# Matmuls of constants, read by nobody, put among the last steps of a layer's mixing stage

## The chip, the cores and the metric

The kernel runs on one core of one Trainium2 chip. The metric is the device time of one execution in microseconds (us). Three executions of the kernel before took 1523.73, 1532.48 and 1538.41 us; the median, 1532.48 us, is the time before.

## The reference

One layer of a hybrid decoder, on 1024 prompt tokens and 8 single tokens that continue older sequences (decode tokens); all tensors are float32. In short:

```
h    = rms_norm(x) ; proj = h @ w_in
y_r  = rwkv7_mix(proj[:, :1792])             # 8 heads of 64: a state matrix per head, updated token by token
y_s  = attention over the last 128 tokens    # 4 query heads, 2 key heads, relative bias, a learned sink
y_m  = attention into 256 memory tokens      # 4 heads
x    = x + concat(y_r, y_s, y_m) @ w_out
x    = x + square(relu(rms_norm(x) @ w_ff1)) @ w_ff2
```

The prompt's attention is computed in blocks of 128 queries. The decode tokens take the same steps with their own state, key and value caches. Outputs are x for all tokens, the new states and the new caches.

## The kernel before

**Stages.** `layers` computes the norm, all projections, the recurrent heads and both attentions, and writes the results of the heads to DRAM (`mixs`); `merge` and `out_proj` load them and multiply by `w_out`; `ffn` does the two large products (`pq` in the trace). Large matmuls split each float32 operand in two parts (tag `w`, `hbig`, `mix`) and take three matmuls for one. The smaller ones are plain float32 matmuls; the trace shows each of these as two MATMUL records.

**The program.** The order of the work in `layers` is written out by hand: the text `PROG` (L35) is a list of steps, and `program` (L407) calls them one after another. `D`, `Q`, `V` are projections. The recurrent heads are 8 units (4 head pairs by 2 halves of the tokens), and each goes through `L F P I W M C N`: load, front, products, inversion of small triangular blocks on GpSimd (L590), values, merge of the inverse (L625), the chain over 8 chunks (L662), and finish (L685; it holds two plain float32 matmuls of 128x128 by 512 columns, `g<-tmp,cst` and `g<-sg,lg`). `A` takes one step of the prompt's attention: 16 steps have work, called units A1 to A16 here. A1 to A8 attend to the memory, A9 to A16 to the window. `R` and `T` take one step of the decode tokens' recurrence (L924) and attention (L1042).

**One attention unit** (`att_unit`, L863) computes the scores of two query blocks in two PSUM buffers of tag `d` (8 matmuls, `d<-mk,qi` and `d<-mkl,qi`, or `d<-kT,qi` and `d<-kTl,qi`), takes the softmax with VectorE and ScalarE, transposes the weights into a buffer of tag `g` (`g<-cst,pe`), copies them out (`pts`) and multiplies with the values. Tag `d` has two buffers, `g` has four, `cx` and `cy` one each (`ps`, L92). A buffer comes free when the last reader of what it held is done.

**Who sets the order.** Each engine executes its own queue in order. The queues are filled by a planner at build time (L1598): a list scheduler that follows a model of the machine, takes the ready instruction that is first in the program, and lets a later one go ahead when an earlier one has to wait for data or for a buffer.

**The decode tokens' attention** uses the tags `cx` and `cy` and two SBUF buffers `d4` (tile `d` in the DMA rows) for its caches, which are loaded one after another.

Of the kernel before, what the change touches and what calls it, by code (L numbers as in the profile page):

```python
# [16 lines left out]
T = 1032  # L17
# [17 lines left out]
PROG = """  # L35
    D12 D13 D8 D0 B G X D4 D6 L0 F0 P0 D5 L1 F1 P1 D10 D1 I0 W0 M0 D9 L2 I1 D2 F2 C0 P2 L3 W1 M1 I2
    C1 N0 F3 P3 D3 W2 M2 L4 N1 F4v P4 C2 D7 I3 V D11 W3 M3 Y I4v Q0 N2 Q1 C3 L5 F5 P5 W4 L6 M4 C4 Q2
    N3 F6v I5 Q3 W5 P6 M5 N4 L7 K C5 F7d A I6 A P7 A W6 M6 R R I7 R R R W7 N5 Av Av C6 Av M7 Av A Av
    N6 C7 T T A T Av T A A N7 A Av Av A R T T T Avc T T
"""  # L40


class K:
# [363 lines left out]
    def program(self, steps):  # L407

        U = [(p, h) for p in range(4) for h in range(2)]
        unit = {"L": self.loads, "F": self.front, "P": self.products, "I": self.invert, "W": self.values,  # L410
                "M": self.merge_inv, "C": self.chain, "N": self.finish}
        self.at = (x for i in (2, 3, 0, 1) for b in range(2) for x in self.attention(i, b))
        self.dt = "cx"
        gen = {"A": self.at, "R": self.decode_rwkv(), "T": self.decode_attn()}
        one = {"B": self.memory, "G": self.bias_tables, "X": self.open_units, "V": self.kv_in, "Y": self.keys, "K": self.open_attn}
        for s in steps.split():
            n = int(s[1:].strip("vdc") or 0)
            self.alt = self.nc.vector if "v" in s else self.nc.gpsimd
            self.gt = "d" if "d" in s else "g"
            self.st = ("cx", "cy") if "c" in s else ("d", "d")  # L420
            if s[0] in unit:
                unit[s[0]](*U[n])
            elif s[0] == "D":
                self.rw_in(n, {12: ("d", "d", "g"), 13: ("cy", "cx", "g")}.get(n, "ddd"))
            elif s[0] == "Q":
                self.q_in(n)
            elif s[0] in gen:
                next(gen[s[0]], None)
            else:
                one[s[0]]()  # L430

    def layers(self):
        self.f = {}
        pool = self.pool
        self.mixs = self.dp.tile([8, 128, TP], F32, name="mixs")
        self.xs = self.dp.tile([12, 128, TP], F32, name="xs")
        self.rk = self.dp.tile([4, 128, TP], F32, name="rk")
        with pool("rows", "left") as self.rp:
            self.xw, self.sg = self.tl("xw", [128, TP]), self.tl("sg", [128, TP])

            self.early = [pool("start", "left"), pool("mem", "left")]
            self.sp = self.early[0].__enter__()
            self.startup()
            self.ep = self.early[1].__enter__()
            self.program(PROG)
            self.apool.__exit__(None, None, None)
            self.dma(self.O["shift"], self.sout)
            self.upool.__exit__(None, None, None)
# [1153 lines left out]
```

## Time and profile before

| | |
|---|---|
| median of 3 runs (lowest, highest) | 1532.48 us (1523.73, 1538.41) |
| profiled execution: its own time, its span | 1522.56 us, 1520.8 us |
| mean granted TensorE clock over the span | 0.919 |
| TensorE matmuls (PE), busy | 1380.5 us, 91% |
| TensorE weight loads (PEld), busy | 1273.3 us, 84% |
| VectorE, GpSimd, ScalarE, busy | 952.4, 754.2, 564.4 us |

The span is the time from the first to the last instruction; 1.8 us of the execution lie around it. The page cuts the span in 40 slices of 38 us and gives, for each, the busy share of each engine in tenths and the TensorE clock that was granted, in tenths of full speed. [...] The attention units, the decode tokens and the last recurrent units run from about 527 to 719 us.

### The profile page before, as it was taken

The numbers are of one execution on the slowest core, as the hardware profiler recorded it, in microseconds if no ns is written. First come the engines' busy times: TensorE is split into PE (matmuls) and PEld (weight loads), VectorE is DVE, ScalarE is ACT, GpSimd is POOL, SyncE is SP. The second block draws the span as 40 slices with busy tenths as digits, with TensorE's granted clock in tenths as the row PEclk, the third lists the DMA queues.
The fourth block names the chain that finished last, engine by engine and source line by source line (L and its number), as shares of the span: only waits on it lengthen the run. The fifth ranks groups of instructions, "written<-read, shape, count | busy, mean of one in ns | idle before, by whom it ended". The sixth has DMA issues, their size and how long they took to land. (4 is left out here: it accounts for less than half of the span.)

```text
span 1520.8 us, 29414 instructions
## 1 busy us (share of the span) xinstructions
PE 1380.5 (91%) x11391; PEld 1273.3 (84%) x11391; DVE 952.4 (63%) x1704; ACT 564.4 (37%) x1057; POOL 754.2 (50%) x905
## 2 busy tenths in 40 slices
PE   5898899989899599896997899999999899999998
PEld 5887797769787477563997799999999899999998
DVE  7658466657766655974446877777777643328830
ACT  6433223223233144343444343344244554423430
POOL 7113563461143655450236565566556555678862
PEclk9899899999889667677998899999999999999999
DMA  6154323314434632336522345545565986469850
GB/s 236 61 164 128 86 71 101 106 49 120 125 108 114 175 82 47 83 100 212 212 84 83 118 173 204 208 165 197 202 215 185 366 319 197 148 221 310 285 168 35
DMA packets 152071, 238.18 MB, mean 157 GB/s; under 512 B 40851, under 2 KB 63340, under 8 KB 151788
## 3 DMA queue, kind: packets, MB, share of 16 engines
q1 hardware_dynamic: 132892, 191.77, 38.7%
q10 hardware_dynamic: 13824, 37.98, 6.8%
q0 software_dynamic: 5216, 6.56, 2.0%
q8 instruction: 89, 1.46, 0.4%
q14 instruction: 50, 0.41, 0.1%
HBM read 165.22 MB, written 72.08 MB: 156 GB/s over the span
## 5 line engine op out<-in xcount | busy, mean ns | idle before, releaser
L85 PE MATMUL pq<-hf,w 128*128 128x258 f32 x2688 | 325.6, 283 | 4.8 <-POOL w L53 2.0
L85 PEld LDWEIGHTS pq<-hf,w 128*128 128x128 f32 x2688 | 324.2, 190 | 6.1 <-POOL w L53 2.5
L53 POOL TENSOR_TENSOR w<-wf,w 128x512 fp32r<-128x512 f32 x130 | 209.0, 1614 | 125.8 <-ACT w L76 112.3
L85 PE MATMUL d<-hbig,w 128*128 128x344 f32 (+2 forms) x1296 | 222.2, 327 | 19.7 <-ACT w L76 9.4
L85 PEld LDWEIGHTS d<-hbig,w 128*128 128x128 f32 x1296 | 202.8, 200 | 32.8 <-ACT w L76 10.6
L53 POOL TENSOR_TENSOR w<-st,w 128x512 fp32r<-128x512 f32 x96 | 153.8, 1630 | 89.2 <-ACT w L76 89.2
L76 ACT CAST w<-wf 128x512 fp32r<-128x512 f32 x190 | 116.6, 617 | 190.2 <-PE pq L85 93.2
L76 ACT CAST w<-st 128x512 fp32r<-128x512 f32 x96 | 59.5, 620 | 222.8 <-DVE st L53 198.3
L53 DVE TENSOR_TENSOR hf<-t,hf 128x1032 fp32r<-128x1032 f32 x56 | 94.0, 1722 | 55.6 <-ACT hf L76 55.6
L53 DVE TENSOR_TENSOR st<-wf,wf 128x512 f32<-128x512 f32 x80 | 85.1, 1073 | 67.6 <-DMA wf<-in_w_ff 59.3
L85 PE MATMUL pq<-xy,w 128*128 128x258 f32 x768 | 103.9, 299 | 18.9 <-DVE t L53 16.4
L85 PEld LDWEIGHTS pq<-xy,w 128*128 128x128 f32 x768 | 101.2, 204 | 22.1 <-DVE t L53 18.3
L53 POOL TENSOR_TENSOR inv<-inv,blk 128x54 f32<-128x54 f32 (+24 forms) x217 | 70.4, 324 | 51.6 <-DMA inv<-in_winit 28.6
L85 PE MATMUL pq<-xe,w 128*128 128x258 f32 x768 | 94.4, 282 | 0.5 <-ACT w L76 0.5
L85 PEld LDWEIGHTS pq<-xe,w 128*128 128x128 f32 x768 | 92.8, 189 | 0.8 <-ACT w L76 0.8
L85 PE MATMUL pq<-xf,w 128*128 128x258 f32 x576 | 76.0, 289 | 9.2 <-DVE xf L53 6.0
L53 POOL TENSOR_TENSOR inv<-inv,inv 128x54 f32<-128x54 f32 (+24 forms) x217 | 75.8, 349 | 15.9
L85 PEld LDWEIGHTS pq<-xf,w 128*128 128x128 f32 x576 | 72.7, 195 | 10.7 <-DVE xf L53 6.8
L53 DVE TENSOR_TENSOR t<-pq,t 128x516 f32<-128x516 f32 x112 | 74.9, 685 | 8.7 <-PE pq L85 7.2
L85 PE MATMUL pq<-xa,w 128*128 128x258 f32 x576 | 73.2, 284 | 2.4 <-DVE t L53 2.4
L85 PEld LDWEIGHTS pq<-xa,w 128*128 128x128 f32 x576 | 71.0, 190 | 2.9 <-DVE t L53 2.8
L73 ACT ACTIVATE t<-t 128x1032 f32<-128x1032 f32 x64 | 67.8, 1065 | 12.2 <-DVE t L53 11.6
(404 smaller groups left out, 2452.9 us busy)
## 6 DMA issues: line engine op xcount, KB each, us to landing
wf<-in_w_ff SPq DMA_DIRECT2D x208, 256.0 KB
t<-hs SPq DMA_DIRECT2D x56, 516.0 KB
hs<-t ACTq DMA_DIRECT2D x48, 516.0 KB
wf<-in_w_in SPq DMA_DIRECT2D x34, 256.0 KB
tmp<-xs SPq DMA_DIRECT2D x32, 256.0 KB
wf<-s2s SPq DMA_DIRECT2D x32, 256.0 KB
x<-in_xT SPq DMA_DIRECT2D x8, 516.0 KB
xs<-xs SPq DMA_DIRECT2D x24, 172.0 KB
```

The costliest lines, as they stand in the source:

```text
L53: return (e or self.nc.vector).tensor_tensor(out, a, b, op=op)
L73: return self.nc.scalar.activation(out, a, f, **k)
L76: return self.nc.scalar.copy(out, a)
L85: return self.nc.tensor.matmul(out, l, r, start=start, stop=stop, **k)
```

## The change

`PROG` gets a new step `J`, put 45 times between the steps from the first `A` to the end, and `J` calls a new function `fill`: one plain float32 matmul of 128x128 by 512 columns. Its operands are columns of `cst`, a tile of constants loaded at the start, and its result goes to a new PSUM buffer of tag `d` that nobody reads.

```diff
-    N3 F6v I5 Q3 W5 P6 M5 N4 L7 K C5 F7d A I6 A P7 A W6 M6 R R I7 R R R W7 N5 Av Av C6 Av M7 Av A Av
-    N6 C7 T T A T Av T A A N7 A Av Av A R T T T Avc T T
+    N3 F6v I5 Q3 W5 P6 M5 N4 L7 K C5 F7d A J I6 J A J P7 J A J W6 J M6 J R J R J I7 J R J R J R J W7 J N5 J Av J Av J C6 J Av J M7 J Av J A J Av J 
+     N6 J C7 J T J T J A J T J Av J T J A J A J N7 J A J Av J Av J A J R J T J T J T J Avc J T J T J 
...
+        one = {"B": self.memory, "G": self.bias_tables, "X": self.open_units, "V": self.kv_in, "Y": self.keys, "J": self.fill, "K": self.open_attn}
...
+    def fill(self):
+
+        self.mm(self.ps("d"), self.cst[:, 0:128], self.cst[:, 0:512])
```

Counted along the text, the fills stand behind the attention units so: 2 behind A1, 2 behind A2, 11 behind A3, then 1, 2, 2, 1, 1, 5, 2, 2, 1, 2, 1, 1 behind A4 to A15, and 9 behind A16. The two `A` after A16 have no work.

## Rows read from the trace of the kernel before

**Rows 1.** The page: busy time of TensorE, and its clock in 40 slices.

```profile
PE 1380.5 (91%) x11391; PEld 1273.3 (84%) x11391; DVE 952.4 (63%) x1704; ACT 564.4 (37%) x1057; POOL 754.2 (50%) x905
...
PEclk9899899999889667677998899999999999999999
```

**Rows 2.** Windows: length; busy (count) of PE, PEld, DVE, ACT, POOL; clock; DMA; GB/s.

```profile
527.85:531.27 3.42, 2.96 (x13) 1.86 (x12) 2.24 (x6) 0.00 (x0) 2.72 (x10) 1.00 0.16 63
531.27:551.75 20.48, 20.48 (x78) 15.25 (x78) 7.35 (x26) 7.41 (x21) 14.94 (x35) 0.50 0.27 69
...
565.40:568.81 3.41, 3.41 (x48) 2.75 (x44) 2.52 (x9) 1.27 (x4) 1.75 (x2) 0.50 0.43 133
...
572.23:592.71 20.48, 20.48 (x119) 17.52 (x121) 7.41 (x21) 5.91 (x23) 13.97 (x46) 0.50 0.10 21
592.71:609.77 17.06, 15.43 (x168) 11.95 (x164) 14.16 (x34) 8.10 (x23) 5.81 (x17) 1.00 0.31 73
609.77:616.60 6.83, 6.83 (x70) 5.50 (x66) 6.58 (x14) 0.64 (x2) 0.72 (x1) 0.50 0.28 77
...
630.25:647.32 17.07, 11.32 (x43) 7.53 (x44) 15.23 (x31) 6.37 (x21) 8.09 (x9) 0.50 0.22 48
647.32:664.39 17.07, 16.93 (x134) 11.72 (x132) 13.93 (x31) 7.25 (x23) 11.51 (x11) 1.00 0.42 125
664.39:681.45 17.06, 16.54 (x78) 11.22 (x77) 12.47 (x62) 9.01 (x28) 8.84 (x11) 0.50 0.36 98
681.45:701.93 20.48, 16.87 (x189) 10.19 (x188) 12.13 (x33) 8.49 (x24) 0.23 (x1) 1.00 0.35 113
701.93:722.41 20.48, 10.82 (x60) 6.08 (x61) 7.01 (x20) 7.03 (x18) 0.00 (x0) 0.50 0.78 280
...
527.85:692.00 164.15, 152.59 (x1169) 112.78 (x1168) 115.05 (x293) 69.60 (x215) 81.75 (x159) 0.74 0.29 76
```

**Rows 3.** TensorE's timeline (start, length): float32 matmuls of 512 columns begun at half clock.

```profile
525.72 2.07 PE L85 MATMUL g<-sg,lg 128*128 128x512 f32 x2
...
590.11 2.02 PE L85 MATMUL g<-tmp,cst 128*128 128x512 f32 x2
592.06 1.43 PE L90 MATMUL g<-cst,y 64*64 64x64 f32 x32
...
646.53 1.42 PE L85 MATMUL g<-tmp,cst 128*128 128x512 f32 x2
...
679.56 1.92 PE L85 MATMUL g<-tmp,cst 128*128 128x512 f32 x2
```

**Rows 4.** The same view: such a matmul at full clock, and what follows it.

```profile
593.42 1.12 PE L85 MATMUL g<-sg,lg 128*128 128x512 f32 x2
594.38 0.33 PE L85 MATMUL cx<-sv,F 128*128 128x64 f32 x2
```

**Rows 5.** The same view: score matmuls at full clock, then at half clock.

```profile
599.21 0.38 PE L85 MATMUL d<-mkl,qi 64*128 64x256 f32 x1
599.52 0.38 PE L85 MATMUL d<-mk,qi 128*128 128x256 f32 x1
...
611.02 0.58 PE L85 MATMUL d<-mk,qi 128*128 128x256 f32 x1
611.53 0.58 PE L85 MATMUL d<-mkl,qi 64*128 64x256 f32 x1
```

**Rows 6.** The same view: A4's scores, a decode step written ahead of A4, A4's transposes.

```profile
555.53 0.38 PE L85 MATMUL d<-mk,qi 128*128 128x256 f32 x1
...
577.15 1.66 PE L85 MATMUL g<-xd,lw 64*128 64x8 f32 x7
...
594.77 1.48 PE L89 MATMUL g<-cst,pe 128*128 128x128 f32 x12
```

**Rows 7.** Timelines of VectorE (A11's scores read) and TensorE (A12's begun).

```profile
646.77 1.66 DVE L70 SCALAR_TENSOR_TENSOR pe<-d,nrq,bias 128x256 f32<-128x256 f32 x4 [1.48 <-PE g L89]
...
649.43 0.36 PE L85 MATMUL d<-kT,qi 128*128 128x256 f32 x1
```

More of the change, by code (lines that the diff above doesn't have):

```diff
@@ L37 @@
     C1 N0 F3 P3 D3 W2 M2 L4 N1 F4v P4 C2 D7 I3 V D11 W3 M3 Y I4v Q0 N2 Q1 C3 L5 F5 P5 W4 L6 M4 C4 Q2
-    N3 F6v I5 Q3 W5 P6 M5 N4 L7 K C5 F7d A I6 A P7 A W6 M6 R R I7 R R R W7 N5 Av Av C6 Av M7 Av A Av
-    N6 C7 T T A T Av T A A N7 A Av Av A R T T T Avc T T
-"""
+    N3 F6v I5 Q3 W5 P6 M5 N4 L7 K C5 F7d A J I6 J A J P7 J A J W6 J M6 J R J R J I7 J R J R J R J W7 J N5 J Av J Av J C6 J Av J M7 J Av J A J Av J
+     N6 J C7 J T J T J A J T J Av J T J A J A J N7 J A J Av J Av J A J R J T J T J T J Avc J T J T J
+ """
 class K:
@@ L414, in program @@
         gen = {"A": self.at, "R": self.decode_rwkv(), "T": self.decode_attn()}
-        one = {"B": self.memory, "G": self.bias_tables, "X": self.open_units, "V": self.kv_in, "Y": self.keys, "K": self.open_attn}
+        one = {"B": self.memory, "G": self.bias_tables, "X": self.open_units, "V": self.kv_in, "Y": self.keys, "J": self.fill, "K": self.open_attn}
         for s in steps.split():
```

## The prediction

> **What bounds the kernel now.** I read the page first, for the clock. TensorE is busy 91% of the span, but its granted clock is well under full in the slices from about 400 to 720 us and at full almost everywhere behind them [rows 1]. The fills are written into the second half of that dip. Then I cut that half into windows at the clock's own changes [rows 2]. From 527.85 us, where A1's scores run, to 692, TensorE is busy 152.59 of 164.15 us; VectorE 115.05, GpSimd 81.75, ScalarE 69.60. So TensorE's queue is the likeliest bound there, and 11.56 us of it are idle.
>
> Six stretches up to 681.45 us run at half clock: 20.48, 3.41, 20.48, 6.83, 17.07 and 17.06 us, of which TensorE is busy 20.48, 3.41, 20.48, 6.83, 11.32 and 16.54, together 79.06 us [rows 2]. The reader is to see two things. In the first four TensorE is busy all the time and yet at half clock: being busy with these small matmuls does not lift it. And the fifth is not TensorE's: VectorE is busy 15.23 of 17.07 us. Behind 701.93 TensorE is busy 10.82 of 20.48 us, and the decode tokens' loads run (DMA share 0.78); that is a tail bound by transfers and their chain.
>
> What lifts the clock is seen in the four matmuls of a fill's form that begin at half clock in this half [rows 3]: they start at 525.72, 590.11, 646.53 and 679.56 us, and the full level begins at 527.85, 592.71, 647.32 and 681.45 [rows 2], 2.1, 2.6, 0.8 and 1.9 us later. Four of four. After them the full level lasted 3.42, 17.06, 17.07 and 20.48 us.
>
> [...] The rows above say that the form of the work counts. [...]
>
> **Where the fills will run.** A fill needs only constants and a buffer, so the planner could run it long before its place in the text. What pins it is the buffer's tag. Buffers of one tag seem to be given out in the order of the text: A4's scores (tag `d`) ran at 555.53 us, ahead of the decode step at 577.15 (tag `g`) that is written before A4, but A4's transposes, in `g` too, came only at 594.77, behind that step [rows 6]. I take the same for `d`: a fill behind A3 runs once A3's scores have been read, and A4's scores wait for all eleven. So the fills come in runs, of 2, 2, 11, 1, 2, 2, 1, 1, 5, 2, 2, 1, 2, 1, 1 and 9, each right behind a read of scores.
>
> **The price of a fill.** At full clock such a matmul takes 0.96 us of the queue (593.42 to 594.38 [rows 4]), at half clock 1.95 (590.11 to 592.06 [rows 3]). No other engine reads the result, and no DMA is issued. 36 fills stand ahead of the tail: 36 x 0.96 = 34.6 us, and 2.0 more for the first two, which I take at half clock: 36.6. The bounds are 34.6 and, if the clock stays as it is (79.06 of 152.59 busy us at half), 36 x (0.52 x 1.95 + 0.48 x 0.96) = 53.1 us.
>
> **What hides of it.** TensorE idles 11.56 us up to 692, 5.75 of them in the stretch at 630.25 [rows 2], where the five fills behind A9 fall: 4.8 us hide there. The rest of the idle time is scattered in small waits ahead of work that is itself late, and a fill that is ready only when scores have been read does not choose its gap: I count nothing more. Bounds: 0 and 11.56.
>
> **What the clock gives back.** A score matmul takes 0.51 us of the queue at half clock (611.02 to 611.53) and 0.31 at full (599.21 to 599.52) [rows 5], as weight loads and sums do not overlap fully; 39% saved, not half. If all 79.06 us were lifted: 30.8 us. The first stretch begins ahead of the first fill, and I leave a third of it (6.8 us) at half: 28.3. Bounds: 0 and 30.8. I stand near the upper end because runs of fills come about every 10 us, and three of the four lifts held 17 us or more.
>
> **The tail.** Nine fills, 8.6 us, become ready together when A16's scores have been read. TensorE idles 3.61 and 9.66 us in the last two windows [rows 2], so I take 0. Bounds: +8.6, if all stand ahead of a decode step that the end waits for, and -4.2, if they hold full clock over the 10.82 busy us. The output projection behind it starts at half clock; that stays.
>
> **The waits for `d`.** Each fill also stands between two units in the only two buffers for scores. At A12 this handover is tight: VectorE ends reading A11's scores at 648.43 us and A12's begin at 649.43 [rows 7]. GpSimd's queue issues the next query loads behind such scores, and holds the attention's multiplications behind those. At A4 it is slack: 39 us lie between its scores and its transposes [rows 6], more than the 10.6 us of its eleven fills. In the sum I count a fill's time in TensorE's queue only, once. Taken alone it is a rival.
>
> **Sum.** 36.6 - 4.8 - 28.3 + 0 = +3.5 us on the profiled execution's 1522.56 us, of which 1520.8 is the span: 1526. That execution lies 9.9 us under the median of the three runs, 1532.48, so on the median the forecast is 1536, no change that can be measured: two sets of runs of this kernel can be told apart from about 1%, 15.3 us.
>
> **Rival 1, slower: the lift does not last.** At 527.85 us full clock came and went in 3.42 us [rows 2]. The fills come in runs, eleven of them at once, and only A1 to A3's runs lie ahead of the busiest half-clock stretch at 572.23 us. If half of the half-clock time stays, the clock gives back 14.2 us, and a quarter of the fills run at half: 36 x (0.75 x 0.96 + 0.25 x 1.95) = 43.5 us. 43.5 - 4.8 - 14.2 = +24.5: 1557. The point from which it is slower by over 1%: the clock's mean from 528 to 692 us, 0.74 before, staying under about 0.89 (gain 19). For it: the lift at 527.85. Against: the three others.
>
> **Rival 2, faster: the fills find room.** Weight loads are busy only 112.78 of 164.15 us [rows 2], and in the score matmuls loads and sums take turns, so part of TensorE's busy time is waiting inside the array; ScalarE and GpSimd would also get their inputs sooner. If two thirds of the 36.6 us hide, 12.2 - 28.3 = -16, and with half of the tail's 4.2, -18: 1514. [...] Against it: fills are queued in order ahead of other work, not dropped into gaps.
>
> **Rival 3: the handover of `d` sets the pace** from A9 to A16. 14 fills stand between these (5, 2, 2, 1, 2, 1, 1), 13.4 us that nothing hides if each unit starts only when its buffers come free; A11's and A15's scores save 8 x 0.2 us each by the clock, 3.2. With the front, where 16 fills (15.4 + 2.0) meet (44.37 - 6.8 + 6.83) x 0.39 = 17.3 us of savings, it is about +10: 1543.
>
> **Rival 4, slower: no lift where TensorE is busy anyway.** Then only the stretch at 630.25 is lifted, 11.32 x 0.39 = 4.4 us, and the fills cost their upper bound: 53.1 - 4.8 - 4.4 = +44: 1576. The four lifts speak against it, three of which came out of windows in which TensorE was busy throughout or nearly so [rows 2, 3].
>
> **Rival 5: the change does not do what it says**, the fills being left out as dead or drawn away from the attention: 1532, same.
>
> **How the numbers follow.** Forecast 0.36, rival 1 0.26, rival 2 0.21, rival 3 0.11, rivals 4 and 5 0.03 each. The forecast's own range, from its bounds on hiding and tail, is 1524 to 1549. Faster by over 1% (under 1517): about 0.7 of rival 2 and 0.15 of the forecast, 0.20. Slower by over 1% (over 1548): 0.8 of rival 1, a seventh of the forecast, a third of rival 3, and rival 4: 0.33. The rest, 0.47, is no change. The range takes in rivals 1 and 2, with 3 us to spare on the one side and 8 on the other: 1511 to 1565. Outside lie rival 4, the clock not lifted at all, 53.1 - 4.8 = +48, and everything won at once, -30.8 - 4.2 = -35.
>
> **What would show it.** The granted clock from 528 to 692 us is to rise from 0.74 to about 0.95; if it is under 0.89, rival 1. The score matmuls in the old half-clock stretches are to take 0.31 us. The fills are to stand in runs as listed, eleven in a row around 555 to 570 us; if they lie elsewhere, the order of the tags is not what I think. TensorE's idle time from A1 to A16 is to fall to about 7 us; more idle time with a later end means the handover of `d` (rival 3), and less busy time than 158 us there means that the fills run beside other work (rival 2). The feed-forward stage must not move: a difference there is none of these.

## The result, and the profile after

The changed kernel took 1549.68 us (median of 4 runs, 1545.61 to 1552.54) beside 1530.17 us for the kernel before: a ratio of 1.0108, with a 95% interval of 1.0068 to 1.0149. A second comparison gave 1.0072 (1.0039 to 1.0104). So it is slower by about 1%, at the edge of the bound that I had set for "no change". The forecast was 1536 us; both medians (1549.68 and 1547.97) lie inside its range and 12 to 14 us above it.

The profiled execution took 1546.97 us (span 1545.2). I call **the stage** the stretch from A1's first score matmul to the first matmul of the output projection (`d<-mix,w`); what lies ahead of it has the same instructions in both kernels. The page of the changed kernel, the lines that answer to [rows 1]:

```profile
PE 1406.3 (91%) x11481; PEld 1278.3 (83%) x11481; DVE 972.6 (63%) x1704; ACT 563.3 (36%) x1057; POOL 765.5 (50%) x905
...
PEclk9899899999887697989999899999999999999999
```

The dip in the clock is shorter: three slices at 7 tenths or less where there were six. The windows of the stage and of what follows it show what that was worth: first two executions of the kernel before, then two of the changed kernel. Columns as in [rows 2].

```profile
527.00:719.00 192.00, 167.32 (x1299) 119.13 (x1298) 121.84 (x324) 77.22 (x241) 82.44 (x161) 0.73 0.34 98
719.00:1520.80 801.80, 759.59 (x5958) 751.52 (x5958) 479.52 (x480) 313.56 (x438) 455.72 (x292) 0.98 0.57 196
```

```profile
534.50:727.80 193.30, 168.69 (x1299) 120.26 (x1298) 122.17 (x324) 77.20 (x241) 82.43 (x161) 0.73 0.34 97
727.80:1530.00 802.20, 759.89 (x5958) 751.70 (x5958) 479.79 (x480) 313.80 (x438) 456.07 (x292) 0.98 0.58 196
```

```profile
533.60:738.80 205.20, 189.65 (x1388) 120.02 (x1387) 123.05 (x323) 77.74 (x240) 81.90 (x161) 0.88 0.31 89
738.80:1545.20 806.40, 763.22 (x5958) 755.19 (x5958) 497.37 (x480) 311.60 (x438) 464.65 (x292) 0.97 0.57 196
```

```profile
533.10:737.00 203.90, 189.08 (x1389) 120.03 (x1388) 122.57 (x324) 77.55 (x240) 81.67 (x161) 0.89 0.31 88
737.00:1545.60 808.60, 761.53 (x5958) 753.61 (x5958) 496.93 (x480) 311.83 (x438) 464.03 (x292) 0.97 0.57 196
```

The reader is to see three things. The stage is 12 us longer (192.0 and 193.3 against 205.2 and 203.9) although its clock rose from 0.73 to 0.88. TensorE is busy about 21 us more there and idle about 9 us less. And the feed-forward part, which has no fill, is 4 to 7 us longer. The first execution of the kernel before starts the stage 7 us earlier than the second one on the same instructions: that is chance, and the first profile was a lucky one, 8 to 10 us under the median of its kernel (1530.17 with the fourth run, 1532.48 without it).

Cut at A16's first score matmul, the stage shows where its 12 us come from, first before, then after:

```profile
527.00:682.00 155.00, 143.59 (x1071) 106.65 (x1070) 106.65 (x277) 65.11 (x202) 82.22 (x160) 0.72 0.30 78
533.60:711.70 178.10, 166.53 (x1239) 108.95 (x1238) 114.07 (x298) 67.79 (x210) 81.67 (x160) 0.87 0.28 77
```

Up to there it is 23.1 us longer, and TensorE's idle time has not changed (11.4 and 11.6 us). The rest of the stage is 9.9 us shorter (37.0 and 27.1 us), and the idle time that went away lies there (13.3 and 4.0 us). A part of both is work that moved: besides the fills, 96 more of TensorE's records stand ahead of A16's scores than before (1239 less the 72 of 36 fills, against 1071).

**The fills.** TensorE's timeline: fills at half clock (0.50 in windows cut at its changes, as in [rows 2]) and at full (1.00), and the pairs between A3 and A4 (a row of x2 is one fill, x4 two).

```profile
542.13 2.02 PE L85 MATMUL d<-cst 128*128 128x512 f32 x2
...
552.75 1.98 PE L85 MATMUL d<-cst 128*128 128x512 f32 x4 [0.27 <-ACT pe L73]
...
561.82 1.98 PE L85 MATMUL d<-cst 128*128 128x512 f32 x4
...
569.18 1.88 PE L85 MATMUL d<-cst 128*128 128x512 f32 x4
...
573.23 1.98 PE L85 MATMUL d<-cst 128*128 128x512 f32 x4
...
576.36 1.98 PE L85 MATMUL d<-cst 128*128 128x512 f32 x4
...
581.20 1.98 PE L85 MATMUL d<-cst 128*128 128x512 f32 x4
...
586.57 2.03 PE L85 MATMUL d<-cst 128*128 128x512 f32 x2
587.61 1.20 PE L85 MATMUL d<-mk,qi 128*128 128x256 f32 x1
```

The price is as read from [rows 3, 4]: two fills in 1.98 us at full clock, one in 2.02 us at half. From the start of each fill to the start of the next instruction, all 45 take 42.4 us (41 begun at full clock, median 0.95; four at half, 1.71), and 42.2 us in the second execution. By this measure a fill right ahead of a score matmul looks short, since the score's record begins inside the fill and lasts longer for it: the one at 623.88 us, shown below, takes 0.61 us to the next one, where [rows 5] have 0.31. Eight fills stand so; with the time by which these scores are late, all 45 take about 44.8 us (45.2 in the second execution).

They stand behind A1 to A16 in the numbers foreseen, but the eleven behind A3 are not in one row: they come in pairs over 25 us, and A4's scores (last line; [rows 6] before) moved from 28.5 to 54.0 us behind A1's.

**A wait that was not there.** M7, the merge of the last inverse, starts the chain of the last recurrent unit. Its matmuls (`g<-inv,ntm`) need VectorE's transposes. VectorE, then TensorE, in the kernel before:

```profile
605.93 0.90 DVE L634 STREAM_TRANSPOSE inv<-W 32x256 f32<-32x256 f32 x2 [0.85 <-DMA W<-ws]
...
606.51 0.22 PE L85 MATMUL g<-inv,ntm 32*32 32x32 f32 x2 [0.39 <-DVE inv L634]
606.89 0.69 PE L85 MATMUL g<-inv,ntm 32*32 32x32 f32 x30 [0.16 <-DVE inv L634]
```

The same in the changed kernel:

```profile
615.39 0.43 DVE L638 STREAM_TRANSPOSE inv<-W 32x256 f32<-32x256 f32 x1
...
622.46 1.98 PE L85 MATMUL d<-cst 128*128 128x512 f32 x4 [1.09 <-ACT pe L73]
623.88 0.68 PE L85 MATMUL d<-mk,qi 128*128 128x256 f32 x1
624.49 0.38 PE L85 MATMUL d<-mkl,qi 64*128 64x256 f32 x1
624.80 0.38 PE L85 MATMUL d<-mk,qi 128*128 128x256 f32 x1
625.11 0.38 PE L85 MATMUL d<-mkl,qi 64*128 64x256 f32 x1
625.81 1.25 PE L89 MATMUL g<-cst,pe 128*128 128x128 f32 x8 [0.32 <-DVE pe L53]
626.99 0.69 PE L85 MATMUL g<-inv,ntm 32*32 32x32 f32 x32
```

Before, TensorE took them as soon as they were there. After, they are ready at 615.82 and begin at 626.99: 11.2 us in TensorE's queue, behind the rest of A6's scores, two fills that wait for a read of scores, and half of A7's. TensorE stands idle for 1.09 us ahead of these fills and does not take M7, which is ready: it keeps to its queue's order here. Between M6's and M7's matmuls the queue holds 16 score matmuls before, and 28 with twelve fills after. The planner had drawn up the order anew: by the two traces, the queues of TensorE, VectorE, ScalarE and GpSimd differ from A2 on (534 to 540 us in the kernel before) and SP's from 611 us on, and all of them also behind the stage.

### The profile page after: what moved, and what is told of

It is laid out like the page before. It is cut to its first block, busy times and chain, and to the rows that moved or that the text cites. A ratio compares the mean times of both kernels' runs of the same rounds, so it can differ in the third digit from the quotient of the medians.

```text
span 1545.2 us, 29545 instructions
## 1 busy us (share of the span) xinstructions
PE 1406.3 (91%) x11481; PEld 1278.3 (83%) x11481; DVE 972.6 (63%) x1704; ACT 563.3 (36%) x1057; POOL 765.5 (50%) x905
## 5 line engine op out<-in xcount | busy, mean ns | idle before, releaser
L85 PEld LDWEIGHTS pq<-hf,w 128*128 128x128 f32 x2688 | 326.8, 191 | 11.2 <-DVE hf L53 3.3
L85 PEld LDWEIGHTS d<-hbig,w 128*128 128x128 f32 x1296 | 204.9, 202 | 32.9 <-ACT w L76 10.3
L53 POOL TENSOR_TENSOR w<-st,w 128x512 fp32r<-128x512 f32 x96 | 161.5, 1707 | 94.5 <-ACT w L76 94.5
L85 PE MATMUL pq<-xe,w 128*128 128x258 f32 x768 | 102.7, 295 | 16.9 <-ACT w L76 9.6
L85 PEld LDWEIGHTS pq<-xe,w 128*128 128x128 f32 x768 | 99.0, 200 | 19.8 <-ACT w L76 11.1
L53 POOL TENSOR_TENSOR inv<-inv,blk 128x54 f32<-128x54 f32 (+24 forms) x217 | 73.7, 340 | 59.1 <-DMA out_state_p<-sl 18.5
L85 PE MATMUL pq<-xy,w 128*128 128x258 f32 x768 | 97.0, 287 | 1.0 <-DVE r L67 1.0
L85 PEld LDWEIGHTS pq<-xy,w 128*128 128x128 f32 x768 | 95.6, 193 | 2.0 <-ACT xy L76 2.0
L73 ACT ACTIVATE t<-t 128x1032 f32<-128x1032 f32 x64 | 67.7, 1064 | 10.2 <-DVE t L53 10.1
```

Of the source, the lines that this page charges most:

```text
L53: return (e or self.nc.vector).tensor_tensor(out, a, b, op=op)
L73: return self.nc.scalar.activation(out, a, f, **k)
L85: return self.nc.tensor.matmul(out, l, r, start=start, stop=stop, **k)
```

## The experiments

Theory 1: the fills' time on TensorE is not paid back by the clock. Theory 2: the place of the other instructions costs, because scores come later, by way of GpSimd (whose query loads wait for scores and hold the inversion behind them) or of the order drawn up anew. Theory 3: chance.

The table has, for each kernel, the ratio to the kernel before with its interval; the stage and its clock in one execution; what the fills take of the queue, from start to the next start, without waits; how long M7's matmuls stand ready; and the time behind the stage.

| kernel | ratio | stage us | clock | fills us | M7 ready us | behind us |
|---|---|---|---|---|---|---|
| before | 1 | 192.0, 193.3 | 0.73, 0.73 | 0 | 0.1 | 801.8, 802.2 |
| changed | 1.0108 (1.0068–1.0149), 1.0072 (1.0039–1.0104) | 205.2, 203.9 | 0.88, 0.89 | 42.4, 42.2 | 11.2, 11.2 | 806.4, 808.6 |
| 2 columns | 1.0053 (1.0028–1.0077) | 212.4 | 0.69 | 14.1 | 19.9 | 797.9 |
| without ten of the eleven | 1.0073 (1.0047–1.0100) | 209.3 | 0.84 | 33.1 | 15.7 | 804.1 |
| the eleven alone | 1.0008 (0.9986–1.0030) | 205.7 | 0.73 | 10.0 | 10.2 | 798.7 |
| bf16 fills | 0.9999 (0.9971–1.0026) | 198.6 | 0.75 | 13.0 | 0 to 2 | 800.3 |
| changed order, fills cut | 1.0071 (1.0037–1.0105) | 199.8 | 0.71 | 5.1 | 12.3 | 806.7 |
| query loads on SP, changed | 1.0084 (1.0057–1.0112) | 205.0 | 0.87 | 43.1 | 18.4 | 807.2 |
| query loads on SP, before | 0.9959 (0.9934–0.9984) | 196.0 | 0.74 | 0 | 0.5 | 804.8 |
| old order, 64 short fills | 1.0108 (1.0080–1.0136) | 220.6 | 0.76 | 34.0 | 2.1 | 802.0 |
| without the fifteen ahead of M7 | 1.0030 (1.0003–1.0057) | 215.1 | 0.79 | 32.6 | 10.0 | 797.4 |
| old order, 32 long fills | 1.0104 (1.0067–1.0141) | 212.5 | 0.80 | 21.9 | 1.9 | 797.6 |

All columns but the ratio are of single executions. Most of these lie within 4 us of their kernel's median; the one with the changed order and the fills cut lies 9 us under it, the one without the fifteen 13 us over it, and the one of the kernel before with the query loads on SP 7 us over it.

**Fills of 2 columns.**

```diff
-        self.mm(self.ps("d"), self.cst[:, 0:128], self.cst[:, 0:512])
+        self.mm(self.ps("d")[:, 0:2], self.cst[:, 0:128], self.cst[:, 0:2])
```

> The 45 fills write 2 columns instead of 512, in the same places and buffers: their time in TensorE's queue is nearly gone, their place in the handover of `d` stays. Theory 1 (TensorE's time: 50.6 us of fills against about 28 us that the clock gave back): nothing is paid and nothing given back, ratio 0.995 to 1.003, mean granted clock of the attention stage back near 0.74, M7's matmuls (`g<-inv,ntm`) within 5 us of the place that they had before, counted from A1's scores (79.5 us). Theory 2 (order and handover: scores come later, GpSimd's query loads wait for them and hold the inversion behind them): still slower, ratio 1.005 to 1.012, GpSimd's waits for scores (`qi <- PE d`) above 33 us (24.3 before, 37.8 after), M7 90 us or more behind A1's scores (93.4 after). Theory 3 (the profile's 13 us are chance): no more than 3 us between this stage and the stage before, with the clock as before.

Measured: 1.0053, GpSimd's waits for scores 62.5 us, M7 99.9 us behind A1's scores. All of it as theory 2 had it, with no gift of the clock at all (0.69).

**The eleven, taken away and left alone.**

```diff
-    ... J W6 J M6 J R J R J I7 J R J R J R J W7 J N5 J Av ...
+    ... W6 M6 R R I7 R R R W7 N5 J Av ...
```

> Ten of the eleven fills between A3 and A4 are left out, the other 35 stay. Theory 2: A4's scores come back to within 5 us of 28 us behind A1's scores (54 after), GpSimd's waits for scores fall below 30 us, M7 stands 76 to 84 us behind A1's scores, ratio 0.996 to 1.004. Theory 1: only 10 x 1.0 us of TensorE's time are gone, and part of the clock's gift with them: ratio 1.004 to 1.009, M7 more than 86 us behind A1's scores. Theory 3: ratio as after, 1.011, and nothing moves.

> The reverse: only the eleven fills between A3 and A4 are there. Theory 2: M7 stays 88 us or more behind A1's scores, GpSimd's waits for scores stay above 33 us, ratio 1.006 to 1.012. Theory 1: eleven fills cost 11 us of TensorE's time and give back at most the half-clock stretch that they lie in (20 us busy x 39% = 8): ratio 0.999 to 1.003, and M7 within 6 us of 79.5 us behind A1's scores.

Without ten of them A4's scores came back to 28.8 us behind A1's, as theory 2 said, but M7 stayed late (88.9) and the time hardly moved (1.0073), as theory 1 said. With the eleven alone M7 is 96.4 us behind A1 and the stage 205.7 us, as theory 2 said, and yet the time is that of the kernel before (1.0008). So the eleven are not the cause by themselves, and neither theory holds by itself; each of the two kernels also has an order of its own.

**bf16 fills.** The operands are columns of a bf16 mask that is mostly ones; 42 of the 45 left a record, one each, where an f32 fill leaves two (90 for 45).

```diff
-        self.mm(self.ps("d"), self.cst[:, 0:128], self.cst[:, 0:512])
+        self.mm(self.ps("d"), self.smask[:, 0:128], self.smask)
```

> The fills take a bf16 constant tile (the mask of ones) for both operands, 128x512, one pass instead of the passes that an f32 matmul takes: nearest row for the price is none, so from both sides, between nothing and the 0.96 us of the f32 fill; places and buffers stay. Theory 1: if the cheap fill lifts the clock as well (mean above 0.85 from A1 to the output projection), the gift stays and the price falls by 20 us or more: ratio 0.985 to 1.000; if it does not lift it (below 0.78), nothing is won or lost: 0.998 to 1.005. Theory 2: order and handover cost as before whatever the clock does, ratio 1.004 to 1.010, M7 88 us or more behind A1's scores.

They cost 0.23 us at full clock and 0.46 at half, did not lift the clock (0.75), and the time did not change: theory 1's "nothing won or lost". Their price is that of the 2-column fills (13.0 and 14.1 us), yet those are 0.5% slower: in each of these kernels the planner drew another order, and that is what the next run holds still.

**The changed order, held, with the fills cut.** The order is drawn up with full fills; then each fill's operands are replaced, so that every queue has the changed kernel's instructions in its order.

```diff
+    shrink(nc, set(k.fl))
...
+                    r, l = x.ins
+                    b.instructions[i] = copy.replace(x, ins=[part(r, 128, 2), part(l, 128, 2)],
+                                                     outs=[part(x.outs[0], 2, 2)])
```

> Every queue keeps the changed kernel's order, instruction by instruction; only the 45 fills are cut, after the order is drawn up, to 2 columns and 2 rows of result. It holds the order and the waits for `d` and takes away TensorE's time and the clock's gift. Theory 1 (TensorE's time, 50.6 us against about 28 given back): the time comes back to before, ratio 0.997 to 1.003, A1 to output projection 190 to 196 us, clock 0.70 to 0.76. Theory 2 (the order): still slow, ratio 1.007 to 1.014, the stage 203 us or more. If the clock's gift is worth more than the fills cost in this order, it is slower than the changed kernel: above 1.012.

> The changed kernel again, with a profile of its own, for the size of chance. If the stage's 205.2 us are its own (theories 1 and 2): 202 to 208 us from A1's scores to the output projection, ratio 1.008 to 1.014. If they are chance (theory 3): below 199 us, or a ratio below 1.006.

1.0071 without the fills' work and 1.0072 with it, in one comparison on one chip. The interval leaves the work 5 us either way. So the changed order is slow without the fills' work: theory 2 in its second form. What the cut fills keep (5.1 us of the queue, their waits for `d`) is not taken apart from it. Theory 3 falls, since the changed kernel repeats its stage (203.9 us) and its time. The stage of this run lies between what the two theories had said (190 to 196 us, and 203 or more). The stage and the rest:

```profile
531.20:731.00 199.80, 180.68 (x1389) 129.97 (x1387) 122.88 (x323) 78.14 (x241) 83.19 (x162) 0.71 0.32 92
731.00:1537.70 806.70, 760.77 (x5958) 752.34 (x5958) 493.37 (x480) 311.38 (x438) 463.94 (x292) 0.97 0.58 195
```

Against the kernel before, the order adds about 7 us in the stage, of which the cut fills can be up to 5.1, and 5 us behind it: in all 7 to 12 us, as the 11 us of the ratio. M7 stands ready from 609.19 and begins at 621.49 (VectorE, then TensorE):

```profile
608.75 0.44 DVE L638 STREAM_TRANSPOSE inv<-W 32x256 f32<-32x256 f32 x1
...
616.36 0.19 PE L85 MATMUL d<-cst 128*2 128x2 f32 x2 [0.17 <-ACT pe L73]
616.47 0.55 PE L85 MATMUL d<-mk,qi 128*128 128x256 f32 x1
...
619.59 1.97 PE L89 MATMUL g<-cst,pe 128*128 128x128 f32 x8 [1.04 <-DVE pe L53]
621.49 1.07 PE L85 MATMUL g<-inv,ntm 32*32 32x32 f32 x32
```

**GpSimd taken out of it.**

```diff
-            self.nc.gpsimd.dma_start(out=q, in_=self.qs[i, :, :, :, t0:t0 + 256].rearrange("h x d t -> (x d) h t"))
+            self.nc.sync.dma_start(out=q.bitcast(F32), in_=self.qs[i, :, :, :, t0:t0 + 256].rearrange("h x d t -> (x d) h t"))
```

> The changed kernel, but the query loads (`qi`) are issued on SP's queue instead of GpSimd's, so that GpSimd no longer waits for scores ahead of the inversion and the attention's multiplications. Theory 2 by way of GpSimd: no wait of `qi` is left in GpSimd's queue, M7 comes 76 to 86 us behind A1's scores (93.4 in the changed kernel), ratio to before 0.996 to 1.005. If GpSimd's wait is beside the path (theory 1, or an order that is late for other reasons): M7 90 us or more behind A1, ratio 1.007 to 1.014.

> The control of that: the kernel before, without fills, with the query loads on SP's queue. If GpSimd's waits for scores (24.3 us before) hold nothing that is late, as I think for the kernel before, ratio 0.995 to 1.003. If the kernel before already loses by them, it is faster: below 0.994.

GpSimd's longest waits (us in total, times, longest), first in the changed kernel, then with the loads on SP:

```profile
POOL qi L858 <- PE d L85: 37.8, 10, 9.5
POOL pe L66 <- PE g L89: 14.3, 5, 5.2
```

```profile
POOL y L53 <- DVE sm L66: 27.5, 3, 26.3
POOL pe L66 <- PE g L89: 24.1, 4, 8.5
```

The wait of `qi` is gone, M7's operands are ready at 610.57 in place of 615.82, and the time is not better: 1.0084. M7's matmuls just stand ready for longer, 18.4 us. So to free GpSimd's queue of these waits does not bring the time back, and theory 2 in its first form falls as far as this run can tell: the planner drew a new order here too (32 score matmuls between M6's and M7's, not 28), and GpSimd then waits elsewhere, up to 26.3 us at once. In the kernel before, the same edit gave 0.9959 (0.9934 to 0.9984), a little better than I thought: it is the one version here that beats both kernels (the kernel before itself, run again, gave 0.9985). The planner drew a new order for it too, so whether the queue or the order earned it is open.

**The old order, held, with fills put in.** The fills enter TensorE's queue after the order is drawn up. First in short form: two of 256 columns behind the first block's scores of each head, into the half of the buffer that is written next.

```diff
+    add_fills(nc, set(k.fl))
...
+            fill = copy.replace(x, name=..., ins=[ap(cst, 256, 0), ap(cst, 128, 0)],
+                                outs=[ap(x.outs[0], 256, 256)], ...)
+            b.instructions.insert(at + 1, fill)
```

> The counterpart of the run that kept the changed order and cut the fills: here every queue keeps the order of the kernel before, and fills are put into TensorE's queue alone after the order is drawn up: two f32 matmuls of constants, 128x256, behind the first block's scores of each head of each of the 16 units (64 in all), into the half of the score buffer that the second block's scores overwrite next. Price: half of a 512-column fill's 0.96 us, about 0.5 us each, 32 us at full clock, an estimate. Theory 2 (the order is what costs; price and gift of the work about cancel): ratio 0.996 to 1.004, M7's matmuls 76 to 84 us behind A1's scores, clock from A1 to the output projection above 0.85. Theory 1 (TensorE's time is not paid back): ratio 1.008 to 1.018.

It is as slow as the changed kernel, with M7 ready for 2.1 us only (97.7 us behind A1's scores, later than theory 2 had it): the work costs by itself here. But the clock stayed at 0.76, so it was no match. Its stage, and the half-clock stretch in which 12 of the 64 fills lie (those of A1 to A3):

```profile
529.20:749.80 220.60, 198.52 (x1427) 141.13 (x1426) 121.60 (x324) 77.59 (x241) 83.38 (x161) 0.76 0.30 86
520.00:567.79 47.79, 44.64 (x188) 32.41 (x189) 16.20 (x46) 10.16 (x31) 27.89 (x71) 0.50 0.29 81
```

Then in the form of the change, one of 512 columns ahead of each head's scores, with the wait of these scores:

```diff
+    add_fills(nc, set(k.fl))
...
+        b.instructions.insert(at, copy.replace(x, name=..., ins=[ap(cst, 512), ap(cst, 128)],
+                                               outs=[ap(x.outs[0], 512)], ...))
```

> The counterpart once more, with fills of the form that lifted the clock in the changed kernel: every queue keeps the order of the kernel before, and after the order is drawn up one f32 matmul of constants, 128x512, is put ahead of the scores of each head of each of the 16 units (32 in all), into the buffer that these scores overwrite. Price at full clock 32 x 0.96 = 31 us (36 of them, 34.6 us, ahead of the tail in the changed kernel). If these fills lift the clock as there (0.88 between A1 and the output projection) and price and gift cancel, so that the order alone made the changed kernel slow: ratio 0.997 to 1.004, M7's matmuls within 2 us of their operands. If the work costs too although the clock rises (theory 1): ratio 1.006 to 1.014. If the clock stays at 0.76 as with the 256-column fills: 1.010 or more, and the placing decides what a fill gives back.

1.0104, clock 0.80, M7 ready for 1.9 us. Here every fill stands right ahead of a score matmul: from start to start they take 21.9 us, and with the time by which these scores are late about 34. TensorE's busy time rose from 168 to 191 us, so the clock gave back only about 11. In the changed kernel, reckoned in the same way, it gave back about 23 of 45. The stage (from the first fill), and a half-clock stretch in which two fills begin:

```profile
537.30:749.80 212.50, 191.17 (x1362) 121.61 (x1360) 121.44 (x323) 77.06 (x241) 82.87 (x160) 0.80 0.31 89
546.39:560.04 13.65, 13.65 (x45) 8.92 (x43) 3.60 (x13) 3.96 (x12) 7.62 (x15) 0.50 0.09 20
```

```profile
549.71 2.02 PE L85 MATMUL d<-cst 128*128 128x512 f32 x2
...
558.91 1.64 PE L85 MATMUL d<-cst 128*128 128x512 f32 x2
```

So a part of theory 1 stands: a fill does not give back the same in every place and order, and set evenly among the scores of the old order it does not pay. The change's own places in the old order were not tried.

**M7 set free, and the kernel before again.**

```diff
-    ... J W6 J M6 J R J R J I7 J R J R J R J W7 J N5 J Av J Av J C6 J Av J M7 J ...
+    ... W6 M6 R R I7 R R R W7 N5 Av Av C6 Av M7 J ...
```

> The changed kernel without the fifteen fills written between A3 and M7 (the run of eleven and the four behind A4 to A6); 30 stay, at A1, A2 and A7 to the end. In its queue 16 score matmuls stand between M6's and M7's matmuls, as in the kernel before (28 and twelve fills in the changed kernel). Theory 2 in the form that M7's ready matmuls stand behind scores: M7 starts within 3 us of its operands (11 after), 76 to 84 us behind A1's scores, ratio 0.997 to 1.004. If the other 30 fills cost by themselves: ratio 1.005 or more although M7 is early.

> The kernel before again, for a second profile: its first profiled execution lies 10 us and more under the median of its runs. If that execution was a lucky one, this one's span lies 5 to 15 us above 1520.8, part of it from A1's scores to the output projection (194 to 200 us in place of 192.0); M7's matmuls start within 1 us of their operands in both. Ratio 0.997 to 1.003, all theories alike.

M7 was not set free: one fill, written behind M7 but drawn ahead of A7's scores, and those scores, ran at half clock ahead of it (the fill's records take 2.08 us, the scores begin 0.51 us apart), and it stood ready for 10.0 us. The time fell to 1.0030 all the same (its stage of 215.1 us is of the execution 13 us over the median, and says little). With the eleven alone (10.2 us, 1.0008) this is the second kernel in which M7 waits and little time is lost. So M7's wait is what the new order looks like in TensorE's queue; that it is the channel by which the order costs is not shown. The kernel before repeated its stage within 1.3 us (ratio 0.9985, 0.9966 to 1.0005).

**What is settled and what is open.** Settled: the changed kernel's order, with what the cut fills keep (5.1 us and their waits for `d`), is as slow as the changed kernel, within about 5 us. The work alone, as 32 or 64 fills set evenly in the old order, is as slow too, since there the clock gives little back (about 11 us of the 32 fills' 34). The two do not add up, because in the changed order the clock gives back most of the price (30.7 of 39.7 us, worked out below). Open: which displaced instruction makes the new order cost.

## Why the prediction was near, and what it left out

**The sum, term by term.** The forecast was made against the kernel before. Price: 45.2 us with the tail's nine (36.6 + 8.6) forecast, 44.8 measured. Gift of the clock: 28.3 forecast, 22.5 measured (167.32 + 44.8 - 189.65; 24.8 in the second pair of executions). Hidden in idle time: 4.8 and the tail's 8.6 forecast, 13.4; idle time falls from 24.7 to 15.5 us, so 9.1 measured, all of it behind A16's first scores: up to there, where the 4.8 were to hide, the sum of the idle time did not fall. Net: 44.8 - 22.5 - 9.1 = +13.2 us in the stage, where the forecast had +3.5, and 4.6 us behind the stage, where it had none. So the forecast had the gift too large by 5.8 us, the hiding by 4.3 and the price by 0.4, and 4.6 us had no term: in all 14.3, about the 12 to 14 us by which the medians lie above it.

With the order held (fills cut against changed kernel), TensorE's busy time without the fills' own time falls from 175.6 (180.68 - 5.1) to 144.9 us (189.65 - 44.8): a gift of 30.7. Idle time falls from 19.1 (199.80 - 180.68) to 15.5 us: 3.6. Net in that frame: 44.8 - 5.1 - 30.7 - 3.6 = +5.4, the step from 199.8 to 205.2 us. So in an order that does not change, the forecast's gift and its +3.5 are of the right size. But that step lies between two single executions, and the medians of these two kernels, 1548.41 and 1547.97 us, do not show it.

**Loads and sums.** The forecast took 39% and not half for a score matmul at full clock, since its weight load and its sums do not overlap fully, and rival 2 built on the same. The trace of the kernel before: TensorE's weight loads of score matmuls, at full and at half clock, and the page's line of the feed-forward part's matmuls.

```profile
599.21 0.18 PEld L85 LDWEIGHTS d<-mkl,qi 64*128 64x128 f32 x1
599.52 0.19 PEld L85 LDWEIGHTS d<-mk,qi 128*128 128x128 f32 x1
...
611.02 0.29 PEld L85 LDWEIGHTS d<-mk,qi 128*128 128x128 f32 x1
611.53 0.29 PEld L85 LDWEIGHTS d<-mkl,qi 64*128 64x128 f32 x1 [0.22 <-issue]
```

```profile
L85 PE MATMUL pq<-hf,w 128*128 128x258 f32 x2688 | 325.6, 283 | 4.8 <-POOL w L53 2.0
```

At full clock the load takes 0.19 of a score matmul's 0.31 us, and 0.12 pass from its end to the next load; a matmul of `pq`, of 258 columns and not 256, takes 0.12 us in all (325.6 us for 2688). At half clock the load takes 0.29 of 0.51 us, and 0.22 pass. So, as an estimate from these rows, loads and sums take turns here (0.19 and 0.12 make the 0.31), and from half to full clock the load falls by about a third, the rest by nearly half.

**What it left out: the order of everything else.** No term of the sum, and no rival, stood for the planner drawing up the queues anew. I wrote that a fill's time counts "in TensorE's queue only, once". Against the kernel before, the gift is only 22.5 us, since the same instructions in the changed order and without fills keep TensorE busy 175.6 us and not 167.3 or 168.7; and the part behind the stage, which I said "must not move", is 4 to 7 us longer, with or without the fills' work.

**A4's slack.** "At A4 it is slack" held eleven fills in a row of 10.6 us against 39 us. The order of the tags was right, and so were all the counts; but the fills ran in pairs over 25 us among other work, so A4's scores came 25 us later and A4 to A7 were pushed together ahead of M7.

**The clock.** Forecast 0.95 from 528 to 692 us; it was 0.84, and 0.88 from the first fill on (542 to 706), as A1 began 7 us later by chance. Both are under the 0.89 which I gave as rival 1's mark. And rival 1's condition held: by the means of 0.73 and 0.88, about 49 of the stage's 104 us at half clock stayed. Its gift (14.2 us) was passed all the same.

The four lifts out of four [rows 3] said too much, in two ways. The clock of the kernel before also rose three times with no matmul of this form in the half-clock stretch ahead:

```profile
551.75:565.40 13.65, 12.83 (x201) 9.81 (x202) 10.09 (x29) 8.42 (x28) 3.98 (x9) 1.00 0.33 69
...
568.81:572.23 3.42, 3.04 (x52) 2.06 (x48) 2.19 (x6) 3.08 (x10) 0.95 (x4) 1.00 0.59 143
...
616.60:630.25 13.65, 11.94 (x92) 8.86 (x88) 11.94 (x16) 7.65 (x23) 8.24 (x8) 1.00 0.43 134
```

And a fill did not always lift it. In the changed kernel the one at 586.57, which ran at half clock but for its first 0.05 us, stands at the start of this stretch:

```profile
586.62:600.27 13.65, 13.65 (x57) 9.20 (x59) 5.05 (x16) 4.30 (x17) 7.81 (x25) 0.50 0.14 30
```

In the run with 32 long fills, a fill begun at half clock at 549.71 did not end its stretch: that lasted to 560.04, 10.3 us later, with TensorE busy for all of its 13.65 us. So neither a matmul of this form nor a TensorE that is always busy was enough for the full clock here; what sets it, no run shows.

**The rivals.** Rival 1 (the lift does not last) came true in its condition, and its 1557 us lie 7 to 9 us above the two medians, where the forecast lies 12 to 14 us below them. Rival 2 (fills find room): from A1 to A16 TensorE is busy 166.5 us, not under 158; it falls, and the idle time up to A16, forecast to fall to about 7 us, stayed at 11.6. Rival 3 (handover of `d`): TensorE's waits for these buffers that the profile lists come to 3.1 us, so the handover on the chip is not the bound, though its +10 us come near the result by another way; its sum also leaves out the six fills behind A5 to A8, 5.8 us. Whether the planner's model of the handover is what spread the eleven fills was not traced. Rival 4 falls with the clock (0.88 in the stage, 0.73 before), rival 5 with the 90 records of fills in their places.

**The chances.** Same 0.47 and slower 0.33: with 1.0108 and 1.0072 the truth lies on the line between them. The mechanism of the forecast was right in kind: the fills lift the clock (0.71 with the fills cut and 0.88 with them, in one order), at the price foreseen (44.8 us, 45.2 forecast). The size was short by what the new order cost, and that it was not further off is in part luck: up to A16's scores the stage grew by 23.1 us and not 3.5, and behind them it shrank by 9.9 us, where I had taken 0 (work that moved ahead is a part of both).

## What to carry to other kernels

Where a planner fills the queues, an added instruction can change the order of all others, even when its own time is paid back: compare the queues of the two programs before pricing the instruction, and give the new order a term of its own. To tell work from order, hold the order: draw it up once, then shrink or insert the instructions in question. Short work meant to keep the clock up paid in no version here (ratios 1.0053 with 2 columns, 0.9999 with bf16, 1.0108 with 256 columns), and what the long fills gave back went from about a third of their price (11 of 34 us) to half (23 of 45) with place and order, so price the gift by place, not by count.

## What the hardware showed beside that

The stage's clock was not the same with fills of other forms and in other places: 0.88 with 45 f32 fills of 512 columns, 0.80 with 32 of them set evenly in the old order, 0.76 with 64 of 256 columns, 0.75 with bf16 fills, and 0.71 and 0.69 with fills of 2 columns, against 0.73 without any. In the run with 64 short fills TensorE stood at half clock for 47.79 us while busy 44.64 of them.

VectorE's instructions in the feed-forward part took longer in the new order, without a change of their own: before and after,

```profile
L53 DVE TENSOR_TENSOR t<-t,r 128x1032 f32<-128x1032 f32 x32 | 45.0, 1406 | 26.6 <-ACT t L73 26.6
```

```profile
L53 DVE TENSOR_TENSOR t<-t,r 128x1032 f32<-128x1032 f32 x32 | 54.6, 1707 | 17.0 <-ACT t L73 16.9
```

With the eleven alone they take 1714 ns too, and the part behind the stage is 798.7 us, so this is not what makes it longer. What goes with it is GpSimd: worked out from the records of both engines, it is busy during 973 ns of a mean one of these 32 before and during 1505 ns after. That the two engines slow one another down here is not shown.
